# Regrouping the first row loads of a batched matmul: fives and two larger transfers instead of fours, fives and sixes

## The chip, the cores and the metric

One core of a Trainium2 chip. The metric is the device time of one execution in microseconds (us), lower is better. All runs named here are of the state "fast". A ratio is the mean time of one kernel's fast runs over that of the other's in the same rounds, so it is not quite the ratio of the medians that are quoted.

## The reference

```python
batch, m, k, n = 32, 512, 1024, 768
x      = np.random.randn(batch, m, k).astype(np.float32)
weight = np.random.randn(batch, k, n).astype(np.float32)
def reference(x, weight):
    return np.matmul(x, weight).astype(np.float32)
```

Everything has to come in (168 MB) and go out (50 MB) once, through 16 DMA engines.

## The kernel before

GpSimd's queue loads the weights and all x but the first, cast to bf16 on the way. The first x comes as float32 on SyncE's queue: three of its four row tiles in one transfer, the last one (`MT - 1`, 128 rows of 4 KB, one for each partition) in many. How many DMA engines a transfer uses depends on its number of rows, so these transfers deal rows out to engines unevenly on purpose.

```python
        x_first = first_pool.tile([P, MT, K], F32)

        nc.sync.dma_start(x_first[:, :MT - 1], x_view[0, :, :MT - 1])
        at = 0
        for few, times in ((4, 2), (5, 1), (6, 1)):
            for _ in range(times):
                for first in range(at, at + 4):
                    rows = slice(first, at + 4 * few, 4)
                    nc.sync.dma_start(x_first[rows, MT - 1], x_view[0, rows, MT - 1])
                at += 4 * few
        for rows in (slice(at, 80), slice(80, P)):
            nc.sync.dma_start(x_first[rows, MT - 1], x_view[0, rows, MT - 1])
        load_w(0)
        # ... identity; loads of batches 1 to 3 ...
        for b in range(B):
            # ... loads ahead; stores of earlier batches, by GpSimd ...
            if b == B - 1:      # the last stores, by SyncE
                halves = [slice(pair * N2, (pair + 1) * N2) for pair in range(2)]
                nc.sync.dma_start(out_view[b - 1, :, halves[0]], outs[b - 1][:, halves[0]])
                for late in range(B - LATE, B - 2):
                    nc.sync.dma_start(out_view[late], outs[late])
                nc.sync.dma_start(out_view[b - 1, :, halves[1]], outs[b - 1][:, halves[1]])
            # ... transposes, matmuls; for the last batch after each half of the rows:
                        if b == B - 1:
                            nc.sync.dma_start(out_view[b, :, halves[pair]], outs[b][:, halves[pair]])
```

SyncE thus makes 19 transfers at the start and 6 at the end, 25 in all.

Of the kernel before, what the change touches and what calls it, by code (L numbers as in the profile page):

```python
# [12 lines left out]
@with_exitstack  # L13
def kernel(
    ctx: ExitStack,
    tc: tile.TileContext,
    x: bass.AP,
    weight: bass.AP,
    out: bass.AP,
):  # L20
    nc = tc.nc
    B, M, K = x.shape
    _, _, N = weight.shape
    P = 128
    MT = M // P
    KT = K // P
    JT = KT // 2
    N2 = 2 * N
    CHUNKED = {B - 4: (4, 4), B - 3: (4, 4), B - 2: (4, 4), B - 1: (4, 2, 2)}
    AHEAD = 3  # L30
    LATE = 4
    HELD = 3

    const = ctx.enter_context(tc.tile_pool(name="const", bufs=1))
    first_pool = ctx.enter_context(tc.tile_pool(name="first", bufs=1))
    w_pool = ctx.enter_context(tc.tile_pool(name="w", bufs=4))
    x_pool = ctx.enter_context(tc.tile_pool(name="x", bufs=5))
    xT_pool = ctx.enter_context(tc.tile_pool(name="xT", bufs=8))
    out_pool = ctx.enter_context(tc.tile_pool(name="out", bufs=7))
    tpsum = ctx.enter_context(tc.tile_pool(name="tpsum", bufs=2, space=bass.MemoryType.PSUM))  # L40
    mpsum = ctx.enter_context(tc.tile_pool(name="mpsum", bufs=2, space=bass.MemoryType.PSUM))



    w_view = weight.rearrange("b (ki ko) n -> b ki ko n", ki=P)
    x_view = x.rearrange("b (mi mo) k -> b mi mo k", mi=P)
    out_view = out.rearrange("b (mi mo) n -> b mi (mo n)", mi=P)

    xs, ws, outs = {}, {}, {}

    def banks():
        return [mpsum.tile([P, 512], F32, name=f"pm{i}") for i in range(3)]

    def load_x(b):
        xs[b] = x_pool.tile([P, MT, K], BF16, name="x_sb")
        nc.gpsimd.dma_start(out=xs[b], in_=x_view[b])  # L56

    def load_w(b):
        ws[b] = w_pool.tile([P, KT, N], BF16, name="w_sb")
        at = 0  # L60
        for n in CHUNKED.get(b, (KT,)):
            nc.gpsimd.dma_start(out=ws[b][:, at:at + n, :], in_=w_view[b, :, at:at + n, :])  # L62
            at += n

    def transpose(b, mt):

        pt = tpsum.tile([P, JT, P], F32, name="pt")
        pairs = xs[b].bitcast(F32)
        for j in range(JT):
            nc.tensor.transpose(pt[:, j, :], pairs[:, mt, j::JT], ident)  # L70
        xT = xT_pool.tile([P, JT, P, 2], BF16, name="xT")
        nc.vector.tensor_copy(  # L72
            xT.rearrange("p j m r -> p (j m r)"), pt.bitcast(BF16).rearrange("p j m -> p (j m)")
        )
        return xT

    def transpose_first(mt):

        xT = xT_pool.tile([P, JT, P, 2], BF16, name="xT")
        for h in range(2):  # L80
            pt = tpsum.tile([P, JT, P], F32, name="pt")
            for i in range(JT):
                nc.tensor.transpose(pt[:, i, :], x_first[:, mt, JT * h + i::KT], ident)  # L83
            nc.vector.tensor_copy(  # L84
                xT[:, 2 * h:2 * h + 2].rearrange("p j m r -> p j r m"),
                pt.rearrange("p (j r) m -> p j r m", r=2),
            )
        return xT



    SPLITS = (
        ((0, 0, 0, 512), (1, 0, 512, N - 512)),
        ((1, N - 512, 0, 1024 - N), (2, 0, 1024 - N, N2 - 1024)),
    )

    def matmuls(pm, half, xT, b, kos, together):
        for ko in kos:
            for i, (bank, at, off, size) in enumerate(SPLITS[half]):
                shares = half == 1 and i == 0  # L100
                nc.tensor.matmul(  # L101
                    pm[bank][:, at:at + size],
                    xT[:, ko // 2, :, ko % 2],
                    ws[b][:, ko, off:off + size],
                    start=(ko == 0 and not (together and shares)),
                    stop=(ko == KT - 1),
                    skip_group_check=together,
                )

    def evacuate(b, pair, pm):  # L110
        o = outs[b][:, pair * N2:(pair + 1) * N2]
        nc.scalar.copy(o[:, 0:512], pm[0])  # L112
        nc.vector.tensor_copy(o[:, 512:1024], pm[1])  # L113
        nc.scalar.copy(o[:, 1024:N2], pm[2])  # L114

    with tc.manual_schedule():
        x_first = first_pool.tile([P, MT, K], F32)

        nc.sync.dma_start(x_first[:, :MT - 1], x_view[0, :, :MT - 1])
        at = 0  # L120
        for few, times in ((4, 2), (5, 1), (6, 1)):
            for _ in range(times):
                for first in range(at, at + 4):
                    rows = slice(first, at + 4 * few, 4)
                    nc.sync.dma_start(x_first[rows, MT - 1], x_view[0, rows, MT - 1])
                at += 4 * few
        for rows in (slice(at, 80), slice(80, P)):
            nc.sync.dma_start(x_first[rows, MT - 1], x_view[0, rows, MT - 1])
        load_w(0)
        ident = const.tile([P, P], F32)  # L130
        make_identity(nc, ident)
        for b in range(1, AHEAD):
            load_x(b)
            load_w(b)
        load_x(AHEAD)

        pending = []
        for b in range(B):
            if b + AHEAD + 1 < B:
                load_x(b + AHEAD + 1)  # L140
            if b + AHEAD < B:
                load_w(b + AHEAD)
            if b <= B - LATE:
                if b > 0:
                    pending.append(b - 1)
                if b + AHEAD < B - HELD or b == B - LATE:
                    for at in pending:
                        nc.gpsimd.dma_start(out=out_view[at], in_=outs[at])  # L148
                    pending = []
# [6 lines that stand above are left out]
            outs[b] = out_pool.tile([P, MT * N], F32, name="out_sb")  # L156
            if b not in CHUNKED:
                turn = transpose if b else lambda _, mt: transpose_first(mt)
                xT = {mt: turn(b, mt) for mt in (0, 1)}
                for pair in range(2):  # L160
                    pm = banks()
                    for half in range(2):
                        if pair == 0:
                            matmuls(pm, half, xT[half], b, range(KT), False)
                            xT[2 + half] = turn(b, 2 + half)
                        else:
                            matmuls(pm, half, xT[2 + half], b, range(KT), False)
                    evacuate(b, pair, pm)
                continue
            xT = {0: transpose(b, 0)}  # L170
            pms = [banks() for _ in range(2)]
            at = 0
            for n in CHUNKED[b]:
                last = at + n == KT
                for mt in range(MT):
                    if mt + 1 not in xT and mt + 1 < MT:
                        xT[mt + 1] = transpose(b, mt + 1)
                    matmuls(pms[mt // 2], mt % 2, xT[mt], b, range(at, at + n), True)
                    if last and mt % 2 == 1:
                        pair = mt // 2  # L180
                        evacuate(b, pair, pms[pair])
                        if b == B - 1:
                            nc.sync.dma_start(out_view[b, :, halves[pair]], outs[b][:, halves[pair]])
                at += n
# [30 lines left out]
```

## Time and profile before

| | before |
|---|---|
| median of the first three runs | 516.93 us (516.87 to 516.96) |
| DMA share of the body | 1.02 |
| TensorE busy | 419.6 us (81%) |
| first transpose / last store issued / last store landed | 33.64 / 501.83 / 513.45 us |

### The profile page before, as it was taken

How to read it: one execution, taken by the hardware profiler on the slowest of the kernel's cores; microseconds unless marked ns; L12 is line 12 of the kernel's file. 1: busy time of each engine (PE TensorE's matmuls, PEld its weight loads, DVE VectorE, ACT ScalarE, POOL GpSimd, SP SyncE). 2: the span in 40 equal slices, each digit the busy share in tenths (PEclk: the TensorE clock that was granted, in tenths of full speed). 3: DMA queues.
4: the chain of work that ended last, by engine and by line, in shares of the span. 5: the costliest groups of instructions: out<-in, count | busy, mean ns of one | idle time of the engine just before them, and what ended most of it. 6: DMA issues, size and time to landing. Idle time of an engine off the chain costs nothing.

```text
span 515.2 us, 6001 instructions
## 1 busy us (share of the span) xinstructions
PE 419.6 (81%) x2576; PEld 275.7 (54%) x2576; DVE 129.8 (25%) x196; ACT 76.2 (15%) x129; POOL 51.7 (10%) x102
## 2 busy tenths in 40 slices
PE   0039999999999988798978879977898978989980
PEld 0026666666666655465645545654564645656650
DVE  0023333333333313133122231322331313332320
ACT  0001111111111101011111111110110111111110
POOL 3000111111000110100101001100111010111000
PEclk9999999999999989799988997998997989999995
DMA  8999999999999999999999999999999999999996
GB/s 233 223 225 220 209 278 277 260 238 276 274 276 267 237 269 276 275 272 245 254 276 275 276 254 243 273 278 275 266 239 265 276 276 274 240 253 213 291 430 272
DMA packets 15081, 135.64 MB, mean 263 GB/s; under 512 B 1744, under 2 KB 1744, under 8 KB 3536
## 3 DMA queue, kind: packets, MB, share of 16 engines
q0 software_dynamic: 13824, 126.88, 96.7%
q1 hardware_dynamic: 1232, 8.39, 4.1%
q8 instruction: 20, 0.33, 0.2%
q14 instruction: 5, 0.04, 0.0%
HBM read 167.77 MB, written 50.33 MB: 423 GB/s over the span
## 4 chain that ended last, share of the span: by engine, by line
DMA 69%; PE 25%; DVE 2%; issue 1%; ACT 0%; POOLq 0%
DMA w_sb<-in_weight_dram 31%; PE pm L101 22%; DMA out_dram<-out_sb 16%; DMA x_sb<-in_x_dram 15%; DMA x_first<-in_x_dram 6%; PE pt L70 2%; PE pt L83 1%; DVE out_sb L113 1%; DVE xT L72 1%; ACT out_sb L112 0%; ACT out_sb L114 0%; POOLq L62 0%; POOLq L148 0%; POOLq L56 0%
## 5 line engine op out<-in xcount | busy, mean ns | idle before, releaser
L101 PE MATMUL pm<-w_sb,xT 128*128 128x256 bf16 (+1 forms) x2048 | 364.7, 336 | 47.9 <-DMA w_sb<-in_weight_dram 44.0
L101 PEld LDWEIGHTS <-xT 128*128 128x128 bf16 x2048 | 203.3, 100 | 184.6 <-issue 50.5
L72 DVE COPY xT<-pt 128x1024 bf16<-128x1024 bf16 x124 | 82.8, 689 | 203.0 <-PE pt L70 203.0
L112 ACT COPY out_sb<-pm 128x512 f32<-128x512 f32 x64 | 37.5, 585 | 286.7 <-PE pm L101 286.7
L70 PEld LDWEIGHTS pt<-ident,x_sb 128*128 128x128 f32 x496 | 72.9, 206 | 6.3 <-issue 1.3
L113 DVE COPY out_sb<-pm 128x512 f32<-128x512 f32 x64 | 44.0, 687 | 128.1 <-PE pm L101 128.1
L70 PE MATMUL pt<-ident,x_sb 128*128 128x128 f32 x496 | 75.4, 286 | 0.0
L114 ACT COPY out_sb<-pm 128x512 f32<-128x512 f32 x64 | 37.5, 586 | 138.2 <-PE pm L101 138.0
L62 POOL DMA_DIRECT2D w_sb<-in_weight_dram x37 | 19.8, 534 | 154.9 <-PE pm L101 74.6
L56 POOL DMA_DIRECT2D x_sb<-in_x_dram x31 | 16.5, 532 | 173.4 <-DMA w_sb<-in_weight_dram 129.4
L83 PE MATMUL pt<-ident,x_first 128*128 128x128 f32 x32 | 6.0, 350 | 33.6 <-DMA x_first<-in_x_dram 33.6
L148 POOL DMA_DIRECT2D out_dram<-out_sb x28 | 15.0, 536 | 93.2 <-DMA x_sb<-in_x_dram 55.9
L83 PEld LDWEIGHTS pt<-ident,x_first 128*128 128x128 f32 x32 | 5.0, 204 | 34.3 <-issue 33.6
L84 DVE CAST xT<-pt 128x512 bf16<-128x512 f32 x8 | 5.6, 726 | 40.7 <-PE pt L83 40.5
L112 ACT ACT_TABLE_LOAD x1 | 1.3, 1283 | 0.7 <-PEq L199 0.7
masks.py:199 POOL TENSOR_SCALAR_AFFINE_SELECT ident<-ident 128x128 f32<-128x128 f32 x1 | 0.3, 287 | 0.1
masks.py:197 POOL MEMSET ident<- 128x128 f32 x1 | 0.2, 223 | 0.0
L199 POOL MEMSET const-float32-0.0<- 128x1 f32 x1 | 0.1, 98 | 0.2 <-issue 0.2
L199 POOL MEMSET const-bfloat16-1.0<- 128x1 bf16 x1 | 0.1, 101 | 0.0
L199 POOL MEMSET const-uint8-127<- 128x1 uint8 x1 | 0.1, 101 | 0.0
L199 POOL MEMSET const-float32-1.0<- 128x1 f32 x1 | 0.1, 98 | 0.0
## 6 DMA issues: line engine op xcount, KB each, us to landing
w_sb<-in_weight_dram POOLq DMA_DIRECT2D x28, 1536.0 KB, 43.2
out_dram<-out_sb POOLq DMA_DIRECT2D x28, 1536.0 KB, 42.0
x_sb<-in_x_dram POOLq DMA_DIRECT2D x31, 1024.0 KB, 39.6
w_sb<-in_weight_dram POOLq DMA_DIRECT2D x7, 768.0 KB, 31.9
out_dram<-out_sb SPq DMA_DIRECT2D x4, 768.0 KB
out_dram<-out_sb SPq DMA_DIRECT2D x2, 1536.0 KB
x_first<-in_x_dram SPq DMA_DIRECT2D x1, 1536.0 KB
w_sb<-in_weight_dram POOLq DMA_DIRECT2D x2, 384.0 KB, 28.6
```

The costliest lines, as they stand in the source:

```text
L56: nc.gpsimd.dma_start(out=xs[b], in_=x_view[b])
L62: nc.gpsimd.dma_start(out=ws[b][:, at:at + n, :], in_=w_view[b, :, at:at + n, :])
L70: nc.tensor.transpose(pt[:, j, :], pairs[:, mt, j::JT], ident)
L72: nc.vector.tensor_copy(xT.rearrange("p j m r -> p (j m r)"), pt.bitcast(BF16).rearrange("p j m -> p (j m)"))
L83: nc.tensor.transpose(pt[:, i, :], x_first[:, mt, JT * h + i::KT], ident)
L84: nc.vector.tensor_copy(xT[:, 2 * h:2 * h + 2].rearrange("p j m r -> p j r m"), pt.rearrange("p (j r) m -> p j r m", r=2),)
L101: nc.tensor.matmul(pm[bank][:, at:at + size], xT[:, ko // 2, :, ko % 2], ws[b][:, ko, off:off + size], start=(ko == 0 and not (together an ...
L112: nc.scalar.copy(o[:, 0:512], pm[0])
L113: nc.vector.tensor_copy(o[:, 512:1024], pm[1])
L114: nc.scalar.copy(o[:, 1024:N2], pm[2])
L148: nc.gpsimd.dma_start(out=out_view[at], in_=outs[at])
L199: nc = _bacc.Bacc("TRN2", target_bir_lowering=False, num_devices=1)
```

## The change

Its intent is to balance the DMA engines otherwise: four engines give up rows, the fifth takes some, and the large transfers go first.

```diff
-        at = 0
-        for few, times in ((4, 2), (5, 1), (6, 1)):
-            for _ in range(times):
-                for first in range(at, at + 4):
-                    rows = slice(first, at + 4 * few, 4)
-                    nc.sync.dma_start(x_first[rows, MT - 1], x_view[0, rows, MT - 1])
-                at += 4 * few
-        for rows in (slice(at, 80), slice(80, P)):
+        few = [slice(at, first + 20, 4) for first in (0, 20, 40) for at in range(first, first + 4)]
+        for rows in (slice(64, P), slice(60, 64), *few):
             nc.sync.dma_start(x_first[rows, MT - 1], x_view[0, rows, MT - 1])
```

SyncE makes 21 transfers instead of 25.

## The prediction

> **What bounds the kernel now.** I read the page's slices first, then its queue table, the stretches, the chain of waits at the end, the timeline at the start, and last the trace's raw record of semaphore increments, because the change moves work among DMA engines and the page only gives their mean.
>
> ```profile
> DMA  8999999999999999999999999999999999999996
> q0 software_dynamic: 13824, 126.88, 96.7%
> q1 hardware_dynamic: 1232, 8.39, 4.1%
> q8 instruction: 20, 0.33, 0.2%
> ```
>
> The 16 DMA engines are busy from the first slice to the last. Queue q0 (weights, x, most stores) fills nearly all of it; q1 is the SyncE queue that the change touches; q8 fetches instructions, 20 pieces of 16 KB.
>
> ```profile
> 40.00:250.00 210.00, 194.80 (x1227) 129.02 (x1225) 61.28 (x93) 35.71 (x61) 22.37 (x43) 0.98 1.02 261
> 505.00:508.00 3.00, 0.00 (x0) 0.00 (x0) 0.00 (x0) 0.00 (x0) 0.00 (x0) 0.50 0.99 416
> 508.00:511.00 3.00, 0.00 (x0) 0.00 (x0) 0.00 (x0) 0.00 (x0) 0.00 (x0) 0.50 0.80 334
> 511.00:515.00 4.00, 0.00 (x0) 0.00 (x0) 0.00 (x0) 0.00 (x0) 0.00 (x0) 0.50 0.09 38
> ```
>
> The last two columns are the DMA share and GB/s. The share is 1.02 (records overlap a little) through the body; after 505 us no compute engine works, and from 508 the share falls to 0.80 and then 0.09: some engines are done and a few, at the end one, are not. That ragged edge is the only room the change has.
>
> ```profile
> 429.20 34.78 DMA w_sb<-in_weight_dram
> 463.98 0.14 issue
> ...
> 501.22 0.58 ACT out_sb L114
> ```
>
> TensorE last waits for data at 464 us, then works through the last three batches by 501.8 us. The last store is issued at 501.83 us and lands at 513.45; the first of its 16 engines lands its share at 508.40, although that share is eight 6 KB packets of 0.22 us, under 2 us of work. So even the engine that is furthest ahead still had about 508.4 - 1.8 - 501.8 = 4.8 us of older transfers in front of it. TensorE is early; the DMA engines set the end.
>
> The increments of a transfer's semaphore, one for each engine, show how far engines lie apart. Behind the first one, in us, sorted:
>
> ```
> landing at 38.90 us:  0 .05 .25 .31 .32 .36 .37 .40 .41 .46 | .73 | 1.34 | 3.03 3.05 3.08 3.19
> landing at 289.26 us: 0 .28 .49 1.41 1.43 1.48 1.68 1.71 1.72 2.40 2.63 2.90 3.04 3.35 3.38 3.85
> landing at 482.69 us: 0 .25 .69 1.72 2.59 2.61 2.67 2.88 2.89 3.03 3.40 3.44 3.51 3.80 4.00 5.04
> last store, 508.40 us: 0 .28 .73 2.33 2.61 2.68 2.86 2.87 3.02 3.38 3.42 3.50 3.79 3.88 3.99 5.05
> ```
>
> An engine never idles, so a lag, once made, stays to the end. One engine ends 5.05 us behind the first and 1.06 us behind the next; it alone sets 513.45 us.
>
> **What the Trainium skill says.** "DMA: Bandwidth & Descriptors", section "Why a DMA increments its semaphore by 16 and not by 1": a transfer runs on the largest k up to 16 that divides its slowest dimension, on SyncE's path on the lowest-numbered k engines, and the sequencer posts the other 16 - k increments at once. So four, five and six rows use engines 0 to 3, 0 to 4 and 0 to 5, one row each; 48 and 64 rows use all sixteen, three and four rows each. The trace agrees in counts: a four-row transfer's semaphore gets four landings beside the sequencer's own, a five-row one five. The same page, section "Queues, rings and completion order", says that an engine takes turns between its queues by packets. The trace agrees: while 12 KB weight packets start 0.907 us apart, successive four-row transfers land 1.98 us apart, which is two such packets (one after the row, one after the row's semaphore write) plus 0.16. "Runtime: NRT & Kernel Launch", section "Instruction fetch mechanics", says instructions are refilled in 16 KB blocks through a DMA queue: here 20 packets of 16,384 B, 0.88 to 0.98 us each. I found no page that says which DMA engine a refill falls on; I read that from the lags.
>
> **The change part by part.** Rows of the last row tile by engine, before. Engines 0 to 3: 8 (fours) + 4 (fives) + 4 (sixes) + 1 (rows 76 to 79) + 3 (rows 80 to 127) = 20; engine 4: 4 + 4 + 3 = 11; engine 5: 4 + 3 = 7; engines 6 to 15: 3 each. Sum 80 + 11 + 7 + 30 = 128. After. Engines 0 to 3: 4 (rows 64 to 127) + 1 (rows 60 to 63) + 12 (fives) = 17; engine 4: 4 + 12 = 16; all others 4. Sum 68 + 16 + 44 = 128. Bytes, requests to compute engines and everything from q0 are unchanged.
>
> The price of a row: the first line of lags has four engines 3.09 us behind on average, with 17 rows more than the ten that lie about 0.31 behind, so (3.09 - 0.31) / 17 = 0.16 us with its semaphore write; 4 KB packets took 172 ns and the next began 19 ns before their end, 0.15. The 1.34 (engine 4, eight rows more) and .73 (engine 5, four more) fit.
>
> Which engine is last? The trace does not number engines, so I followed each lag from landing to landing. The four at 3.03 to 3.19 are engines 0 to 3. The q8 refills each push one lag up by about 1.1 us, in a cycle of eight: the first, ninth and seventeenth (at 49.9, 222.1, 423.7 us) take engine 5 from .73 to 1.81, 2.91 and 3.99; the other seven victims come from engines 6 to 15. Smaller 8 KB refills on q14, at 119.7, 294.2 and 476.3 us, take one of engines 0 to 3 from 3.19 to 3.85, 4.52 and 5.04; two more (148.0, 205.1) take two of its neighbours to 3.40 and 3.44. Engine 4 takes no q8 refill and ends at 1.72. So the last engine is one of 0 to 3.
>
> New lags on the same scale, as estimates: last engine 5.04 - 3 x 0.16 = 4.56; its neighbours 2.6 to 3.0; engine 4 1.72 + 5 x 0.16 = 2.5; engine 5 4.00 - 4 x 0.16 = 3.4; engines 6 to 15 one row more, the highest 3.88 + 0.16 = 4.04. The largest is still 4.56, so the end moves by -0.48 us. Nothing else is on that path: four transfers fewer save SyncE some 0.66 us of issue each, early and beside everything.
>
> Start of TensorE:
>
> ```profile
> 0.74 0.38 SPq L119 DMA_DIRECT2D x_first<-in_x_dram  x1
> 1.18 20.43 SPq L125 DMA_DIRECT2D x_first<-in_x_dram  x16
> 22.69 2.31 SPq L128 DMA_DIRECT2D x_first<-in_x_dram  x2
> ...
> 33.64 1.73 PE L83 MATMUL pt<-ident,x_first 128*128 128x128 f32 x7 [33.64 <-DMA x_first<-in_x_dram]
> ```
>
> The first transpose waits for the last strided transfer (33.55 us), not for the two contiguous ones behind it (35.02 and 38.46). That was 16 x 2 = 32 turns of engines 0 to 3 after the big first transfer. Afterwards the contiguous ones come first and the last five ends after 5 + 2 + 24 = 31 turns with one row more: 0.61 us (an 8 KB packet of q0) less, 0.15 more. I expect about 33.1 us. It does not count: TensorE has the slack shown above.
>
> **The rivals.** First: an engine that gets more becomes last. For it: thirteen lags lie above 1.7, and eleven engines gain work. Against it: the highest among engines 6 to 15 would need over four rows more to be last ((4.56 - 3.88) / 0.16), and gets one. If I took engine 4 for the wrong lag, and it is the one at 4.00, it would end at 4.8 and the gain shrink to 0.25 us: 516.7. Second: refills fall elsewhere, because SyncE's program is four instructions shorter or the fetches meet other packets; a 0.66 us refill more or less on an engine of the 0-to-3 group makes 515.8 to 517.1. For it: the last engine owes 1.85 us of its lag to three refills. Against it: TensorE's program, which causes the q8 fetches, is the same. Third: the start moves the end, by way of a late first transpose. For it: the path from the transposes to the refilling of buffers waits on TensorE early (a 34.93 us wait of GpSimd, ended at 50.90). Against it: transfers issued before that wait land until 63.97 us, so the queue has over ten microseconds in hand; and my count makes the start earlier. It would make 517 or a little more only if the fives landed 10 us later. Fourth: fewer, larger transfers win by themselves, as "DMA: Bandwidth & Descriptors", section "Rules for kernel authors", advises against small ones. Here the small ones interleave with full-rate q0 packets and cost an engine only their bytes and a 22 ns semaphore packet, four of them less: below 0.1 us.
>
> **Range and chances.** 516.93 - 0.48 = 516.45 us. The three runs before span 0.09 us; the rivals reach from 515.8 to 517.1, the likelier part 516.15 to 516.95. No reading of the lags gives more than about 1 us either way (the gap to the next engine is 1.06), while 2% is 10.3 us, so faster or slower by that is next to excluded.
>
> **What would show it.** In the trace after: at the landing near 39 us, five engines some 2.1 to 2.6 us behind in place of four at 3.1; a first transpose near 33.1; the last store's slowest increment near 513.0 with the next about 0.5 before it; DMA share still 1.02 in the body. I am wrong if the last lag is not in the group that lost three rows (then the end stays or moves by +0.16), or if q14's refills move to another engine.

## More of the kernel before

The lines on which the argument rests stand in the prediction. One more, which the prediction did not look at, is of SyncE's waits (who waited for what: us in total, times, longest):

```profile
SPq L210 <- DMA out_dram<-out_sb: 11.2, 2, 7.8
```

L210 is the end of the program. SyncE waits there for the stores, and found only two of its waits unfulfilled.

## The result, and the profile after

Before 516.92 us (six runs, 516.87 to 516.96), after 516.37 us (six runs, 516.29 to 516.76). The ratio is 0.999 with a 95% interval of 0.9978 to 1.0003; the medians differ by 0.55 us. With an interval of some 0.6 us either way, what is said below of tenths of a microsecond rests on the traces, with the medians beside them. A trace is of one execution: the one of the kernel before took 517.03 us, 0.11 more than its median, the one of the changed kernel 516.39.

The DMA lines of the page after, and the stretches of the body and the end:

```profile
DMA  8999999999999999999999999999999999999997
q0 software_dynamic: 13824, 126.88, 96.9%
q1 hardware_dynamic: 1216, 8.39, 4.1%
```

```profile
40.00:250.00 210.00, 192.58 (x1210) 127.48 (x1209) 60.63 (x93) 35.12 (x60) 22.81 (x43) 0.98 1.02 261
505.00:508.00 3.00, 0.00 (x0) 0.00 (x0) 0.00 (x0) 0.00 (x0) 0.00 (x0) 0.50 0.98 412
508.00:511.00 3.00, 0.00 (x0) 0.00 (x0) 0.00 (x0) 0.00 (x0) 0.00 (x0) 0.50 0.87 365
511.00:515.00 4.00, 0.00 (x0) 0.00 (x0) 0.00 (x0) 0.00 (x0) 0.00 (x0) 0.50 0.08 34
```

The body is as full as before. From 508 to 511 us the DMA share is 0.87 instead of 0.80: the engines end closer together. q1 has sixteen packets fewer: four transfers fewer, with one semaphore write for each engine they used. The start and the chain of waits:

```profile
0.74 0.38 SPq L119 DMA_DIRECT2D x_first<-in_x_dram  x1
1.19 20.24 SPq L122 DMA_DIRECT2D x_first<-in_x_dram  x14
...
33.25 3.03 PE L83 MATMUL pt<-ident,x_first 128*128 128x128 f32 x12 [33.25 <-DMA x_first<-in_x_dram]
```

```profile
428.79 34.78 DMA w_sb<-in_weight_dram
463.57 0.14 issue
...
500.82 0.58 ACT out_sb L114
```

The first transpose comes at 33.25 us, 0.39 earlier. The last wait of TensorE for data ends 0.41 us earlier (463.57 for 463.98) and so does the last eviction.

From the trace's record of semaphore increments, as in the prediction (behind the first engine, in us, sorted):

```
after, landing at 39.13 us:  0 .06 .08 .26 .32 .36 .37 .39 .43 .44 .56 | 1.96 | 2.23 2.23 2.30 2.34
after, landing at 484.08 us: 0 .05 .12 .81 1.07 1.39 1.42 1.45 1.46 1.52 1.54 1.70 2.17 2.33 2.57 3.27
after, last store, 509.78:   0 .10 .17 1.09 1.40 1.41 1.48 1.49 1.53 1.58 1.71 2.17 2.33 2.60 2.78 3.27
```

Engine 4, which the prediction feared it had taken for the wrong lag, is the 1.96 of the first line and, since the first engine itself fell back meanwhile by 1.16 us against the kernel before, the .81 of the second: no refill hit it.

The last store lands at 513.05 us, 0.40 us earlier. But the span is 0.64 us shorter (514.60 for 515.25). The other 0.24 us lies behind the landing. SyncE's waits at the end, after:

```profile
SPq L204 <- DMA out_dram<-out_sb: 11.0, 5, 3.4
```

Five of the waits at the end now took time instead of two. SyncE walks through its eight DMA semaphores, which the framework gives its transfers in turn, in a fixed order, 0.061 us apart where nothing is left to wait for. Before, transfer 25 used the first of them: the wait ended at 513.47, and seven fulfilled ones followed until 513.90. After, transfer 21 uses the fifth: the wait ended at 513.07, and three followed. From the landing to the end of SyncE's walk the traces have 0.575 us before and 0.333 after; 4 x 0.061 = 0.24.

### The profile page after: what moved, and what is told of

It is laid out like the page before. It is cut to its first block, busy times and chain, and to the rows that moved or that the text cites. A ratio compares the mean times of both kernels' runs of the same rounds, so it can differ in the third digit from the quotient of the medians.

```text
span 514.6 us, 5996 instructions
## 1 busy us (share of the span) xinstructions
PE 418.7 (81%) x2576; PEld 275.4 (54%) x2576; DVE 129.7 (25%) x196; ACT 76.2 (15%) x129; POOL 51.7 (10%) x102
## 4 chain that ended last, share of the span: by engine, by line
DMA 62%; PE 31%; DVE 3%; issue 1%; SPq 1%; ACT 0%; POOLq 0%
DMA w_sb<-in_weight_dram 32%; PE pm L101 28%; DMA out_dram<-out_sb 16%; DMA x_sb<-in_x_dram 8%; DMA x_first<-in_x_dram 6%; PE pt L70 2%; DVE out_sb L113 1%; DVE xT L72 1%; PE pt L83 1%; SPq L122 1%; ACT out_sb L114 0%; SPq L119 0%; POOLq L142 0%; POOLq L62 0%; POOLq L56 0%
```

## The experiments

My theory after the result: two sums, rows (-0.40 us) and place in the list (-0.24 us). Rivals: it is all rows; or a difference of chip and hour; later also: an earlier start, or the number of transfers as such. Twelve traces, all correct:

| kernel | rows of engines 0-3 / 4 / 5 / others | place in list | last landing | landing to end of walk | median |
|---|---|---|---|---|---|
| before | 20 / 11 / 7 / 3 | 1 | 513.45 | 0.575 | 516.92 |
| after | 17 / 16 / 4 / 4 | 5 | 513.05 | 0.333 | 516.37 |
| again (after) | 17 / 16 / 4 / 4 | 5 | 513.29 | 0.323 | 516.59 |
| index_7 | 17 / 16 / 4 / 4 | 8 | 512.98 | 0.145 | 516.11 |
| index_0 | 17 / 16 / 4 / 4 | 1 | 512.91 | 0.574 | 516.60 |
| old_rows_index_4 | 20 / 11 / 7 / 3 | 5 | 513.51 | 0.328 | 516.75 |
| fives_first | 17 / 16 / 4 / 4 | 5 | 513.09 | 0.334 | 516.52 |
| heavier | 23 / 11 / 5 / 2 | 5 | 516.07 | 0.328 | 518.90 |
| heavier_early | 23 / 11 / 5 / 2 | 5 | 513.84 | 0.323 | 517.16 |
| one_transfer | 8 / 8 / 8 / 8 | 8 | 514.55 | 0.140 | 517.09 |
| fourteen | 14 / 14 / 8 / 5 | 8 | 513.87 | 0.140 | 516.84 |
| before_again | 20 / 11 / 7 / 3 | 1 | 513.32 | 0.574 | 516.97 |

The kernel before, timed beside them on the same chips, stayed at 516.93 to 516.95. The traced execution isn't always near the median: it was the slowest of its five in heavier (519.38) and one_transfer (517.67) and the fastest in index_0 (516.48).

**again**: the changed kernel, no edit.

> The changed kernel itself, once more, so that the others of this call have it on the same chip. Theory: the -0.55 us of the first measurement is two sums. The last store lands 0.40 us earlier (513.05 for 513.45) because the last DMA engine has three rows less; and after it SyncE, which walks through its eight DMA semaphores in a fixed order at 0.061 us each, has three left instead of seven, because the last store is transfer 21 of SyncE and not 25: 4 x 0.061 = 0.24. Expected here -0.5 to -0.6 us against before, with both parts again in the trace. Rival (all rows, no second part): the same time, but a landing 0.5 to 0.6 earlier. Rival (chance of one chip): a difference that is not there again.

516.59 us (516.37 to 516.88), -0.34 against before at a ratio of 0.9994 (0.9981 to 1.0006). Smaller than expected; the walk is again 0.25 shorter, but the landing gained only 0.16 us. In this trace the last engine is 0.31 us ahead of its place in the kernel before from the landing near 50 us on, where it was 0.64 ahead in the first trace. So the last engine's place at the start differs by 0.3 us from one execution to another; in the first 9 us 12 KB packets of x took up to 2.0 us where 0.47 is the rule, which is the likely cause but was not tested. The other 0.15 us went at about 430 us, where four weight packets are stretched.

**index_7**, edit to the changed kernel:

```diff
-        for rows in (slice(64, P), slice(60, 64), *few):
+        for rows in (*[slice(at, at + 16) for at in range(64, P, 16)], slice(60, 64), *few):
```

> The changed kernel with rows 64 to 127 as four transfers of 16 instead of one of 64: every DMA engine has the same rows, SyncE makes 24 transfers in all instead of 21, so the last store uses the last semaphore of the list. Theory: 3 x 0.061 = 0.18 us faster than the changed kernel, about -0.73 against before. Rival (rows alone decide): the same as the changed kernel, or slower by a few hundredths for the three transfers more.

**index_0**, the same with, in addition:

```diff
                 for late in range(B - LATE, B - 2):
+                    if late < B - LATE + 1:
+                        for half in halves:
+                            nc.sync.dma_start(out_view[late, :, half], outs[late][:, half])
+                        continue
                     nc.sync.dma_start(out_view[late], outs[late])
```

> As index_7, with one of the late stores also cut in two halves: 25 transfers, the last store uses the first semaphore of the list, as in the kernel before. Theory: 7 x 0.061 = 0.43 us slower than index_7 and 0.24 slower than the changed kernel, about -0.3 against before. Rival (rows alone decide): the same as index_7 within 0.1.

Medians 516.11 (515.97 to 516.85) and 516.60 us (516.48 to 516.86): 0.49 apart where 0.43 was expected, though single runs of the two overlap. SyncE's waits at the end, of index_7 and then of index_0:

```profile
SPq L204 <- DMA out_dram<-out_sb: 10.6, 5, 2.7
```

```profile
SPq L208 <- DMA out_dram<-out_sb: 11.3, 2, 10.3
```

With place 8 the last waits end one by one and none is left behind the landing (0.145 us to the end); with place 1 seven are left (0.574). Index_0's last store even landed 0.07 us earlier than index_7's, so the difference is the list. It also speaks against "fewer transfers": index_7 makes three more than the changed kernel and its median is lower. The next run is clearer: it makes four transfers more than the kernel before, and all its five times lie below all nine of that.

**old_rows_index_4**, edit to the kernel before (and both late stores in halves):

```diff
-        for rows in (slice(at, 80), slice(80, P)):
+        for rows in (slice(at, 80), slice(80, 96), slice(96, 112), slice(112, P)):
```

> The kernel before with its old rows on every engine, but rows 80 to 127 as three transfers of 16 and both late stores in halves: 29 transfers, the last store uses the fifth semaphore, as in the changed kernel. Theory: the landing stays at about 513.4 and only the list is shorter, -0.24 us against before. Rival (rows alone decide): the same time as before.

```profile
SPq L214 <- DMA out_dram<-out_sb: 11.1, 6, 3.0
```

516.75 us (516.72 to 516.83), -0.18 against before. Landing 513.51, as with the old rows; walk 0.328, with six waits at the end that took time where the kernel before had two. The list alone is worth about 0.2 us without any row moved.

**fives_first**, edit to the changed kernel:

```diff
-        for rows in (slice(64, P), slice(60, 64), *few):
+        for rows in (*few, slice(60, 64), slice(64, P)):
```

> The changed kernel's rows and number of transfers, with the twelve fives first, then the four, then the 64. Theory: the first transpose waits for the last five, now after 24 turns instead of 31, so TensorE starts some 5 us earlier (near 28 us), and the end does not move: within 0.2 us of the changed kernel on this chip (about 516.4 to 516.6). Rival (the order or the earlier start is worth something): more than 0.3 us either way.

TensorE started at 29.03 us, 4.2 us earlier, and the end stayed: landing 513.09, median 516.52 us (516.41 to 517.05) beside 516.59 of again. Neither the order nor the earlier start is worth anything that these runs show.

**heavier**, the other way, edit to the kernel before:

```diff
-        for few, times in ((4, 2), (5, 1), (6, 1)):
+        for few, times in ((4, 3), (5, 1), (6, 1)):
             for _ in range(times):
-                for first in range(at, at + 4):
-                    rows = slice(first, at + 4 * few, 4)
+                count = 3 if few == 6 else 6 if few == 5 else 4
+                for first in range(at, at + count):
+                    rows = slice(first, at + count * few, count)
                     nc.sync.dma_start(x_first[rows, MT - 1], x_view[0, rows, MT - 1])
-                at += 4 * few
-        for rows in (slice(at, 80), slice(80, P)):
-            nc.sync.dma_start(x_first[rows, MT - 1], x_view[0, rows, MT - 1])
+                at += count * few
+        nc.sync.dma_start(x_first[at:P, MT - 1], x_view[0, at:P, MT - 1])
```

> The other way: engines 0 to 3 get 23 rows of the last row tile instead of the 20 of before (12 fours, 6 fives, 3 sixes and one transfer of 32), engine 4 keeps 11, engine 5 gets 5, the others 2. 29 transfers, so the last store uses the fifth semaphore of the list, as in the changed kernel. Theory (one of engines 0 to 3 lands last, 0.16 us a row): landing 3 x 0.16 = 0.48 later than before, list 0.24 shorter: about +0.24 us against before, landing near 513.9, and a last-store spread near 5.7. Rival (the last engine is one of 6 to 15): landing 0.16 earlier than before, -0.4 us in all.

518.90 us (518.50 to 519.38), ratio 1.0039 (1.0026 to 1.0051): 1.7 us over what I expected. The first transpose waits for all strided transfers, and those now ended at 42.5 us. GpSimd's timeline and the stretch after it, of heavier:

```profile
59.99 0.53 POOL L62 DMA_DIRECT2D w_sb<-in_weight_dram  x1 [44.06 <-PE pm L101]
```

```profile
60.00:62.00 2.00, 1.65 (x12) 1.12 (x12) 1.48 (x3) 0.31 (x1) 1.05 (x2) 1.00 0.93 154
62.00:66.00 4.00, 4.00 (x28) 2.58 (x27) 0.69 (x1) 0.59 (x1) 0.00 (x0) 1.00 1.00 203
```

and of the kernel before, in which the same weight load could be issued at 50.90 us:

```profile
50.90 0.53 POOL L62 DMA_DIRECT2D w_sb<-in_weight_dram  x1 [34.93 <-PE pm L101]
```

```profile
60.00:62.00 2.00, 2.00 (x15) 1.22 (x13) 0.00 (x0) 0.59 (x1) 0.00 (x0) 1.00 1.12 236
62.00:66.00 4.00, 3.69 (x26) 2.56 (x25) 1.97 (x3) 0.58 (x1) 1.06 (x2) 1.00 0.99 210
```

The transfers issued earlier reach their end on the first engine at 60.61 us in heavier (60.78 in the kernel before). A weight load issued at 59.99 comes only 0.62 us ahead of that, where the kernel before had 9.9: the DMA share dips to 0.93 and the rate to 154 GB/s, and then 66 weight packets between 61.2 and 71.0 us are stretched by 27.7 us in all, 27.7 / 16 = 1.73 us for each engine, in a trace whose last store lands 2.62 us late. With the 0.39 us that three rows cost in the next run, about 0.5 us of that stays unexplained.

**heavier_early**, edit to heavier: the same numbers of rows, taken contiguously.

```diff
+        for few in (4,) * 12 + (5,) * 6 + (6,) * 3 + (32,):
+            rows = slice(at, at + few)
+            nc.sync.dma_start(x_first[rows, MT - 1], x_view[0, rows, MT - 1])
+            at += few
```

> The rows of heavier (23 on engines 0 to 3) and its 29 transfers, but each small transfer takes contiguous rows, so that the first transposes wait for the first big transfer alone and TensorE starts near 15 us instead of 42.6. Theory: heavier missed its +0.24 by 1.7 us because its late first transpose put the fifth weight load off to 59.99 us, when the leading engines ran dry at about 60.8, and not because of its rows. Then here no burst of slow weight packets near 61 us, and the +0.24 us of the rows and the list: near 517.2. Rival (23 rows on four engines do cost 2 us, whatever the start): near 518.9, as heavier.

517.16 us (517.14 to 517.17), +0.21; landing 513.84, +0.39 for three rows more; no burst. TensorE started at 10.30 us. GpSimd's timeline of heavier_early:

```profile
53.55 0.53 POOL L62 DMA_DIRECT2D w_sb<-in_weight_dram  x1 [37.32 <-PE pm L101]
```

So rows on the last engine cost 0.13 us each in the other direction too, a little under the 0.16 of the prediction, and heavier's 1.7 us went with its late start. That the burst of stretched packets comes of running dry is argued, not shown: fourteen below has bursts although its weight loads were issued some 44 us before they landed.

**one_transfer**, in place of all the small transfers:

```diff
+        nc.sync.dma_start(x_first[:, MT - 1], x_view[0, :, MT - 1])
```

> The last row tile as one plain transfer of 128 rows, 8 on each engine: no balancing at all. 8 transfers, the last store uses the last semaphore of the list. Theory: the last engine of before gets 12 rows less and leads; now those of engines 6 to 15 with three instruction refills are last (3.88 behind in the kernel before, five rows more): 3.88 + 0.80 = 4.68 on that scale, so landing near 513.1, list 0.43 shorter than before: about -0.8 us, 516.1 to 516.3. TensorE starts near 15 us instead of 33 and that is worth nothing. If extra slow weight packets come with smaller spreads (as in all four kernels with the new rows), up to 0.3 more. Rival (the balancing is worth what its author thought, the fours, fives and sixes beat the plain transfer): over 517.5.

517.09 us (516.79 to 517.67): a miss, 0.8 to 1.0 over the estimate. TensorE started at 10.25 us, which was worth nothing. In the trace, of the slowest execution, the last engine landed 514.55, not 513.1. As expected it is not one of engines 0 to 3 any more, but one that takes instruction fetches: its lag rises by 1.0 to 1.2 us each after the first, ninth and seventeenth fetch (32.5, 222.3 and 424.6 us); some 1.6 us more came in smaller steps that I could not attribute. Its fetches are not the ones I had counted on: the durations, which repeat in a cycle of eight, begin 975, 962, 893, 893, 949 ns here and 893, 878, 948 ns in the kernel before, so the cycle began at another engine. That also happened between the two traces of the changed kernel (893, 885, 948 and 975, 949, 893, 893, 948).

**fourteen**: 14 rows each on engines 0 to 4.

```diff
+        whole = [slice(at, at + 16) for at in (80, 96, 112)] + [slice(48, 80)]
+        sixes = [slice(at, 48, 3) for at in (30, 31, 32)]
+        for rows in (*whole, *sixes, slice(25, 30), slice(0, 25)):
+            nc.sync.dma_start(x_first[rows, MT - 1], x_view[0, rows, MT - 1])
```

> Rows chosen from the lags: 14 each on engines 0 to 4, 8 on engine 5, 5 on the others; 16 transfers, last semaphore of the list. Theory: the last of engines 0 to 3 falls by 3 x 0.16 from the changed kernel, to about 512.6, and the next, of engines 6 to 15, rises by 0.16 to about 512.7, which is then the end: 0.35 us less than the changed kernel, and 0.18 from the list: about 515.9 to 516.1, the fastest so far. Rival (the balance is already as good as the start-up scatter of 0.3 us lets it be): the same as index_7, 516.1, or slower.

516.84 us (516.80 to 517.10), nothing gained. The estimate left out stretched weight packets. Taking 12 KB weight packets of over 926 ns between 40 and 440 us, those just behind an instruction fetch left out:

| kernel | such packets | us over 926 ns, all engines |
|---|---|---|
| before; before_again; old_rows_index_4; heavier_early | 2 each | 0.38; 0.30; 0.25; 0.14 |
| one_transfer | 7 | 0.96 |
| after; again; index_7; index_0; fives_first | 17; 17; 19; 28; 32 | 2.78; 2.91; 2.41; 3.26; 3.58 |
| fourteen | 52 | 13.19 |
| heavier | 68 | 28.06 |

In fourteen the packets come in bursts, the largest at 240.7 to 243.4 and 413.9 to 416.9 us; 13.19 / 16 = 0.82 us for each engine, about the distance between the landing I expected (512.7) and the one seen (513.87), with 0.35 left over. I do not know what stretches them. It is not simply that engines run close together: in one_transfer the eight leading ones lie within 0.4 us of each other at the landing near 135 us, where it is 1.3 in fourteen and 1.4 in the changed kernel, and it has few.

**before_again**: the kernel before, no edit.

> The kernel before, once more with a trace. Theory: the cycle of 16 KB instruction fetches begins on another DMA engine in each execution (it did in the second trace of the changed kernel), but never on engines 0 to 3, whose 20 rows make one of them last; so the landing stays within 0.1 us of 513.45 and the times within 0.2 us of each other, while kernels with 17 rows or fewer there scatter over 0.4 to 0.9. Rival (the scatter belongs to the chip or the hour, not to the rows): a spread of 0.4 us or more here too.

516.97 us (516.86 to 517.01); landing 513.32, 0.13 earlier, a little more than I had allowed. The cycle of fetches began at the same engine as in the first trace, so this run did not test the first part of the expectation. The second held: the times of both kernels with 20 rows and of heavier_early with 23 lie within 0.03 to 0.22 us of each other, those of the kernels with 8 to 17 rows on engines 0 to 3 within 0.3 to 0.9 (as do those of heavier, with its burst: 0.9). That fits last engines with and without instruction fetches, but only the profiled executions have traces, so it is not shown run by run.

**A version that beats both.** Index_7, with 516.11 us, is the fastest by median: 0.82 us under the kernel before of its rounds (ratio 0.9987, 0.9975 to 1.0), 0.48 under the changed kernel on the same chip. Even so it is within 2%.

## Why the prediction was right or wrong

The time was right (516.45 said, 516.37 measured), and the mechanism was one that it named: the DMA engines set the end, and the one that is last lost rows. That it came within 0.08 us is luck: the rows gave less than said, and a second term that the prediction had not seen made up for it. By its own steps:

- *The last engine is one of 0 to 3, and each of its rows costs 0.16 us.* Right, but for the size. Three rows fewer moved the landing by -0.40, -0.16, -0.47, -0.54 and -0.36 us in the five traces with the new rows, -0.39 on average, where -0.48 was said; three rows more moved it by +0.39 (heavier_early). That is 0.13 us a row. All are counted from the first trace before; from the mean of its two (513.45 and 513.32) they are 0.07 us less and more. The term was 0.1 us too large on average, within the 0.3 us that the start scatters.
- *Nothing else is on that path; four transfers fewer are worth below 0.1 us.* Wrong. The walk through the semaphores behind the last landing became 0.24 us shorter, since the last store moved from place 1 to place 5. Old_rows_index_4 has that part alone (-0.18 us by medians), index_7 and index_0 vary it alone (0.49). The two errors had opposite signs: about -0.4 and -0.24 gave -0.63 in the traces, and -0.55 and -0.34 in the medians.
- *Engines 6 to 15 shift by one row, 0.16.* Wrong for the leading ones: the first engine of the last store came 1.38 us later, not 0.16, so the spread fell to 3.27 and not to 4.4. It was 0.22 us late from the landing at 39.13 us on, about the row; the rest came in steps after 240 us. Stretched weight packets, 2.78 us over all engines after 40 us, account for 0.15 us of an engine's mean delay. One packet, stretched by 0.24 us at 338.4 us, comes where the last engine's gain falls from 0.62 to 0.40. Why the packets come with the new rows stays open.
- *First transpose near 33.1 us and without effect.* Right that it has no effect: fives_first moved it by 4.2 us, one_transfer by 23, with nothing to show for it. The time itself was 33.25 in the first trace, but 33.59 in again and 33.52 in before_again, so the half microsecond that the count of turns gave isn't shown.
- *A late start needs 10 us to matter, and then makes 517 or a little more.* About right as a threshold: heavier's start is 8.9 us later, and the first engine of the kernel before has 60.78 - 50.90 = 9.9 us in hand (the prediction's 63.97 is the last engine, not the first). The size was too small: 1.7 us, with a burst of stretched packets.
- *Refills fall elsewhere.* Named as a rival, and it is real: the cycle begins at different engines in different executions. It did not decide this comparison: in these two traces the cycle began alike (893, 878, 948 and 893, 885, 948 ns), and the last engine was one that the fetches of the cycle spare.

## What to carry to other kernels

When DMA engines are full from start to end, read when each engine lands its share of the last transfers: only the one that is last counts, and a row moved away from it is worth its own transfer time and no more. Then look past the last landing: the order in which the program waits for its semaphores at the end may leave fulfilled waits behind the last one, and the number of transfers made at the start can decide that. A balance tuned to tenths of a microsecond should be tried over several executions, because the engines that instruction fetches hit were not always the same here.

## What the Trainium skill lacked or had wrong

- "Runtime: NRT & Kernel Launch", section "Instruction fetch mechanics", says that the cost of crossing a 16 KB block is mostly hidden. For the DMA engine that carries the block it was not: each of the 20 fetches took 0.88 to 0.98 us and put one engine back by about 1.1 us, in a kernel that the DMA engines bound. The page does not say which engines carry them: here by the lags a cycle of eight, none of them engines 0 to 4, which began at different places in different executions.
- No page that I found tells of the walk through the DMA semaphores at a program's end: 0.061 us for each fulfilled wait, 0.14 to 0.575 us in all from the last landing to its end, by the place of the last transfer's semaphore.
- "DMA: Bandwidth & Descriptors" has no word on weight packets that are stretched in the middle of a full queue: 926 ns as a rule, up to 2,232 ns in heavier, and 2 or 68 stretched packets in a run depending on how 128 rows were dealt out at the start.
